# The second MLP product of a two-layer trunk with its seven block products as the outer loop

## The chip, the cores and the metric

The kernel runs on one core of a Trainium2 chip. The metric is the device time of one execution in microseconds, the median of three plain runs of the kernel before. A profiled execution of its own gives the trace.

## What is computed

The reference is a trunk of two residual layers over 1024 tokens of width 1024 in float32. Each layer is a mixer (gated DeltaNet and GLA in the first, Mamba-2 SSD and RWKV-7 in the second) followed by an MLP with a squared ReLU; a last RMSNorm ends it.

```python
for layer in range(DEPTH):                      # DEPTH = 2, D_MODEL = 1024, D_FF = 4096
    hn = _rmsnorm(h, norm_mix_w[layer])
    ...                                         # mix = even or odd mixer of hn
    h = h + mix.astype(h.dtype)
    h = h + _sqrelu_mlp(_rmsnorm(h, norm_mlp_w[layer]), mlp_w1[layer], mlp_w2[layer]).astype(h.dtype)
return _rmsnorm(h, final_norm_w)

def _sqrelu_mlp(h, w1, w2):
    return jnp.square(jax.nn.relu(h @ w1)) @ w2
```

The change is in the second product of the MLP, (1024 x 4096) times (4096 x 1024), in both layers, and in the normalisation that follows it.

## The kernel before

The program is written with a tile framework: tiles come from pools with a number of buffers for each tag, dependencies become semaphore waits, and the order of each engine's instructions is fixed when the program is built, by a list scheduler that goes by program order and by priority. Code in `with self.urgent()` gets the highest priority. Each engine executes its instructions in that order, and a waiting instruction holds all that stand behind it on its engine. All DMAs are issued from the SP queue, in order too (`load` and `store`, L156).

The second product uses a seven-product block scheme (Strassen-Winograd). The output, tokens by columns, is cut into 2 x 2 blocks of 512 x 512, and so are the factors: the contraction over 4096 rows is cut into halves (z in `down_rows`, alternating blocks of 128 rows). The left factors of the seven products, sums and differences of halves of the activations, were made by the first product (`up`) and lie transposed in DRAM as `d_s` (7 x 16 x 128 x 512). The right factors are the quarters of W2 (`quads`, tile tag w2) and, for products 5, 6, 7 and 4, running differences of them, made on VectorE in `right` (L1815), two instructions of 128 x 1024 each.

The contraction inside one block product, 2048 rows, is taken in four parts of 512 rows (b). One pair (b, i) is 48 matmuls of 128 x 128 by 128 x 512: 4 slices of 128 rows, 4 tiles of 128 tokens, 3 terms. The three terms come from the splitting of each float32 factor into a rounded high part and a remainder: `down_splits` (L1737) makes a tile of tag hn for each factor with one ScalarE cast and one VectorE difference for each of its two halves, urgent. The pool hn has four buffers, so two products' factors.

Before the change b is the outer loop (L1807) and the seven products, in the order 1, 2, 5, 6, 3, 7, 4, are the inner one. A PSUM group a (four banks of tag pm) sums products 1, 6, 7 and 4 of one b, a group c (two banks of tag pd and two of tag pt) takes 2, then 5 and 3. After each product `add` (L1793) adds the four banks on VectorE to a 512 x 512 block of h, which is in SBUF as eight tiles: four of tag hh, four of tag acc. Quarters of W2 are loaded once for each b, four loads of 1 MB, and the left factors seven times 1 MB; each 1 MB is two DMAs of 512 KB. sr has two buffers, w2 five.

The stage begins while `up` still runs. `down_start` (L1749) loads the factors of the first product, the raw left factor of the second (`early`) and two tiles of h. The pools of `down` (w2, sr, acc) lie where `up` had its own, so their loads wait for it. They then go out in this order (L1835 to L1850): right factor of product 2, two quarters, left factor of product 5, a quarter of h, left factor of product 6, a quarter of W2, the rest of h.

At the end (b = 3) the last product, 4, goes tile by tile through `seven` (L1537), and the generators `done` (L2047) finish the eight token tiles: the sum of squares (made by `add`), `rms` (its power on POOL, L188), the scaling by row and column, the store. In layer 0, `done` also transposes the normalised tile on TensorE in banks of tag pt and splits it for the next layer. In layer 1, `weigh` multiplies half of a tile by the norm's weights on POOL beforehand.

Of the kernel before, what the change touches and what calls it, by code (L numbers as in the profile page):

```python
# [8 lines left out]
FP32 = mybir.dt.float32  # L9
# [10 lines left out]
NT = SEQ // 128  # L20
# [19 lines left out]
class Trunk:  # L40
# [1708 lines left out]
    def down_start(self, W2, d_s, d_h, out):  # L1749

# [15 lines left out]
        out.extend((raw, h))  # L1766
        yield

    def down(self, M, W2, d_s, d_h, begun, weigh, done):


        *begun, h = begun
        for t in range(2, NT):
            h.append(self.big() if t < 4 else M[2].tile([128, D], FP32, tag="acc", name=self.name("acc"), bufs=4))
        rows = self.down_rows(W2)
        order = (1, 2, 5, 6, 3, 7, 4)

        def raw(m, src):
            t = fresh(m)
# [4 lines left out]
        def fresh(m):  # L1784
            tag, bufs = (("sr", 2), ("w2", 5))[m]
            return M[1 - m].tile([128, 4, 512], FP32, tag=tag, name=self.name(tag), bufs=bufs)

        split = self.down_splits
        ahead = {}

        ss = self.const.tile([128, NT, 2], FP32, tag="ssq", name=self.name("ssq"))

        def add(half, c, ps, last, tiles=range(4)):  # L1793
            for tt in tiles:
# [4 lines left out]
                if last:  # L1799
                    self.sum_sq(ss[:, t, c:c + 1], v)  # L1800
                    if half and c:
                        weigh(v)

        for b in range(4):
            quad = {}

            def quads(z, c):  # L1807
                if (z, c) not in quad:
                    quad[z, c] = raw(1, rows[b, z][:, :, c * 512:c * 512 + 512])
                return quad[z, c]  # L1810

            def left(i):
                return raw(0, d_s[i - 1, 4 * b:4 * b + 4].rearrange("j p t -> p j t"))

            def right(i):  # L1815
                if i in (1, 2, 3):
                    return quads(*((0, 0), (1, 0), (1, 1))[i - 1])
                if i == 5:
                    quad["x"] = fresh(1)
                    src = quads(0, 1), quads(0, 0)  # L1820
                elif i == 6:
                    src = quads(1, 1), quad["x"]
                elif i == 7:
                    src = quads(1, 1), quads(0, 1)
                else:
                    src = quads(1, 0), quad["x"]
                out = quads(0, 1) if i == 7 else quad["x"]
                for j in range(0, 4, 2):
                    self.tt(out[:, j:j + 2], src[0][:, j:j + 2], src[1][:, j:j + 2], SUB)
                return out  # L1830

            a = [self.pm() for _ in range(4)]
            c = None
            for n, i in enumerate(order):
                if not b and not n:  # L1835
                    def rest(half, q):
                        for t in range(max(2, 4 * half), 4 * half + 4):
                            cs = slice(q * 512, q * 512 + 512)
                            self.load(h[t][:, cs], d_h[t * 128:t * 128 + 128, cs])

                    l, r, early = begun
                    right(2), quads(0, 0), quads(0, 1)
                    ahead[5] = left(5)
                    rest(0, 0)
                    ahead[6] = left(6)
                    quads(1, 1)
                    for half, q in ((1, 1), (0, 1), (1, 0)):
                        rest(half, q)
                elif not b and n == 1:
                    l, r = split([early, right(2)])  # L1850
                else:
                    l, r = split([ahead.pop(i, None) or left(i), right(i)])
                if i in (2, 5):
                    c = [self.pd(), self.pd(), self.pt(), self.pt()]
                ps = c if i in (2, 5, 3) else a
                new = i in (1, 2, 5)
                if b == 3 and i == 4:
                    ends = [done(t, h[t], ss[:, t]) for t in range(NT)]
                    for e in ends[0:4]:
                        next(e)  # L1860
                    for tt in range(4):
                        self.seven(c[tt], l, r, 4, True, slice(tt * 128, tt * 128 + 128))
                        next(ends[tt], None)
                        add(1, 0, c, True, (tt,))
                        next(ends[4 + tt])
                    for e in ends[4:8]:
                        next(e, None)
                    continue
# [237 lines left out]
```

## Time and profile before

| | us |
|---|---|
| median of three plain runs | 2613.86 (2611.11 to 2621.36) |
| profiled execution | 2596.22 |
| its span, first to last instruction | 2594.5 |
| mean granted TensorE clock | 0.983 |
| second product, layer 0 | from about 912 to 1250 |
| second product, layer 1 | from about 2263 to the end |

The profile's page gives the busy time of each engine over the span; a table of stretches gives the same for any part of it, with the granted clock and the share and rate of the DMA engines. In a timeline each row is a run of like instructions, with its start, its duration and, in brackets, how long its engine had been idle before it and what ended that. A busy TensorE is not one at its peak, since matmuls overlap: the distance of their starts tells the pace.

### The profile page before, as it was taken

Reading aid. Unit: us, or ns where it says so; the run is one execution under the profiler, and the core shown is the slowest. Engines: PE = TensorE matmul, PEld = TensorE weight load, DVE = VectorE, ACT = ScalarE, POOL = GpSimd, SP = SyncE. Lnnn points to the kernel's source line nnn. Section 1 sums busy time; section 2 is a strip of 40 time slices with the busy share of each in tenths; the row PEclk is TensorE's granted clock in tenths of the full one; section 3 lists DMA queues with packets and bytes.
Section 4 is the critical chain, followed back from the end, with each engine's and each line's share of the span. In section 5 each row is a group of like instructions: output and inputs, shape, how many; then the busy total and the mean of one; then the engine's idle time right before and its main releaser. Section 6 shows DMA issues by size and latency. Waiting matters only on the chain. (4 is left out here: it accounts for less than half of the span.)

```text
span 2594.5 us, 39524 instructions
## 1 busy us (share of the span) xinstructions
PE 2495.4 (96%) x14230; PEld 2080.4 (80%) x14230; DVE 1756.8 (68%) x3033; ACT 1131.5 (44%) x2131; POOL 538.2 (21%) x546
## 2 busy tenths in 40 slices
PE   7999999999999989999899999998999999999998
PEld 6788898997787768887677788887897778778886
DVE  6677443447687778778366558777657677777877
ACT  5732344336544533334343333444437444533334
POOL 2020124302344200001031112245211434100001
PEclk9999999999999999999999899999999999999999
DMA  4556544645766674442235356667646766674432
GB/s 141 155 154 181 158 157 149 220 152 157 230 226 229 223 268 159 161 146 95 77 94 173 108 171 185 194 194 211 198 143 189 226 229 211 217 263 162 144 132 98
DMA packets 428965, 452.75 MB, mean 175 GB/s; under 512 B 55153, under 2 KB 301154, under 8 KB 428770
## 3 DMA queue, kind: packets, MB, share of 16 engines
q1 hardware_dynamic: 428770, 450.23, 54.2%
q8 instruction: 113, 1.85, 0.3%
q14 instruction: 82, 0.67, 0.1%
HBM read 304.84 MB, written 145.28 MB: 173 GB/s over the span
## 5 line engine op out<-in xcount | busy, mean ns | idle before, releaser
L161 PE MATMUL pd<-hn,whi 128*128 128x512 f32 x1216 | 409.8, 411 | 1.4 <-DVE cy L184 1.1
L161 PE MATMUL pd<-whi,hn 128*128 128x256 f32 (+2 forms) x2048 | 394.3, 289 | 6.7 <-ACT hn L171 4.0
L161 PEld LDWEIGHTS pd<-whi,hn 128*128 128x128 f32 x2048 | 322.6, 190 | 13.2 <-ACT hn L171 4.4
L1873 PE MATMUL pm<-hn,hn 128*128 128x512 f32 x1440 | 330.4, 389 | 0.0
L1873 PEld LDWEIGHTS pm<-hn,hn 128*128 128x128 f32 x1440 | 270.1, 188 | 56.8 <-DVE x L177 0.6
L161 PE MATMUL pd<-wlo,hn 128*128 128x256 f32 (+2 forms) x1024 | 294.7, 288 | 0.3 <-DVE wlo L177 0.2
L161 PEld LDWEIGHTS pd<-hn,whi 128*128 128x128 f32 x1216 | 224.1, 190 | 53.9 <-issue 7.8
L161 PE MATMUL pd<-hn,wlo 128*128 128x512 f32 x608 | 248.2, 408 | 0.0
L171 ACT CAST hn<-sr 128x1024 fp32r<-128x1024 f32 x104 | 108.7, 1047 | 316.1 <-PE pm L1873 181.3
L188 POOL TENSOR_TENSOR rs<-rs,mhalf 128x1 f32<-128x1 f32 x40 | 22.8, 571 | 883.1 <-DVE rs L177 671.0
L161 PEld LDWEIGHTS pd<-wlo,hn 128*128 128x128 f32 x1024 | 194.4, 190 | 2.3 <-DVE wlo L177 0.9
L177 DVE TENSOR_TENSOR wlo<-wst,whi 128x512 fp32r<-128x512 f32 (+2 forms) x172 | 122.8, 718 | 84.2 <-ACT whi L171 75.9
L171 ACT CAST whi<-wst 128x512 fp32r<-128x512 f32 (+2 forms) x172 | 106.5, 620 | 165.7 <-PE pd L161 121.5
L1537 PE MATMUL pm<-rf,whi 128*128 128x512 f32 x512 | 161.4, 396 | 10.1 <-DVE h L177 10.0
L1873 PE MATMUL pd<-hn,hn 128*128 128x512 f32 x576 | 150.5, 396 | 14.4 <-ACT hn L171 11.5
L1537 PE MATMUL pm<-hn,whi 128*128 128x512 f32 x512 | 162.9, 399 | 0.9 <-ACT whi L171 0.9
L1873 PE MATMUL pt<-hn,hn 128*128 128x512 f32 x576 | 149.2, 394 | 0.0
L1873 PEld LDWEIGHTS pd<-hn,hn 128*128 128x128 f32 x576 | 109.7, 192 | 40.1 <-ACT hn L171 12.8
L177 DVE TENSOR_TENSOR hn<-sr,hn 128x1024 fp32r<-128x1024 f32 x104 | 127.0, 1221 | 16.3 <-ACT hn L171 16.2
L161 PEld LDWEIGHTS pd<-hn,wlo 128*128 128x128 f32 x608 | 115.2, 189 | 28.2 <-issue 3.6
L177 DVE TENSOR_TENSOR hn<-w,hn 128x1024 fp32r<-128x1024 f32 x108 | 131.4, 1218 | 4.5 <-ACT hn L171 4.5
L1873 PEld LDWEIGHTS pt<-hn,hn 128*128 128x128 f32 x576 | 109.8, 191 | 23.2
(430 smaller groups left out, 4998.5 us busy)
## 6 DMA issues: line engine op xcount, KB each, us to landing
sr<-d_s SPq DMA_DIRECT2D x104, 512.0 KB
hh<-in_mlp_w_dram SPq DMA_DIRECT2D x64, 512.0 KB
d_s<-s SPq DMA_DIRECT2D x128, 256.0 KB
w<-in_mlp_w_dram SPq DMA_DIRECT2D x64, 512.0 KB
d_s<-x SPq DMA_DIRECT2D x64, 256.0 KB
hh<-d_rec SPq DMA_DIRECT2D x32, 512.0 KB
wst<-in_even_w_in_dram SPq DMA_DIRECT2D x56, 256.0 KB
wst<-in_odd_w_in_dram SPq DMA_DIRECT2D x52, 256.0 KB
```

The lines of the kernel that those rows point to most:

```text
L161: self.nc.tensor.matmul(out=out, lhsT=lhsT, rhs=rhs, start=start, stop=stop)
L171: self.nc.scalar.copy(out=out, in_=in_)
L177: (eng or self.nc.vector).tensor_tensor(out=out, in0=a, in1=b, op=op)
L188: self.nc.gpsimd.tensor_tensor(out=out, in0=in_, in1=self.mhalf.broadcast_to(list(in_.shape)), op=ALU.pow)
L1537: self.nc.tensor.matmul(out=ps, lhsT=wt[l][:, k, sl], rhs=x[r][:, k, :], start=start and k + j == 0, stop=k + j == n + 1, skip_group_check ...
L1873: self.nc.tensor.matmul(out=ps[tt], lhsT=l[x][:, k, sl], rhs=r[y][:, k, :], start=new and k + q == 0, stop=k + q == 5, skip_group_check=True)
```

## The change

The seven block products become the outer loop and the four parts b the inner one. A block product is summed over all four parts in PSUM (`start` only at b = 0), and only then added to h, or, for product 5, copied by ScalarE into four tiles u5 (buffers of tag wlo), to which product 7's group is added.

- Since b is inside, each quarter of W2 is loaded again for each block product that uses it: 36 loads of 1 MB a layer in place of 16; the left factors stay at 28. Product 5's differences are kept on chip in four tiles (tag x) for products 6 and 4, product 7's is made in place in a w2 buffer.
- One pool takes the place of three: sr 2, w2 3 and x 4 buffers of 8 KB a partition.
- h is no longer loaded at the start. `fetch` loads its first four tiles behind the third part of product 1, and the other four, into two x tiles, behind the second part of product 4, where u5 and the sums a are then added.
- The first four token tiles are finished (`done`) behind product 3 and no longer in the last product. In both layers the scaling is done in place, except for the half that `weigh` multiplied on POOL, now in layer 0 too (tiles 4 to 7). In layer 0 the store of h goes before the scaling, and the transposes of tiles 0 to 3 use banks of tag pm.

```diff
-    def down_start(self, W2, d_s, d_h, out):
+    def down_start(self, W2, d_s, out):
...
-            self.load(raw[-1], d_s[1, j:j + 2].rearrange("j p t -> p j t"))
-        h = [self.big() for _ in range(2)]
-        for i, x in enumerate(h):
-            self.load(x, d_h[i * 128:i * 128 + 128])
+            self.load(raw[-1], d_s[0, 4 + j:6 + j].rearrange("j p t -> p j t"))
...
+        def right(i, b):
+            quad = lambda z, c: raw("w2", rows[b, z][:, :, c * 512:c * 512 + 512])
+            if i in (1, 2, 3):
+                return quad(*((0, 0), (1, 0), (1, 1))[i - 1])
+            if i == 5:
+                src = quad(0, 1), quad(0, 0)
+                out = xs[b] = fresh("x")
+            elif i == 7:
+                src = quad(1, 1), quad(0, 1)
+                out = src[0]
+            else:
+                src = quad(1, 1 if i == 6 else 0), xs[b]
+                out = xs[b]
+            for j in range(0, 4, 2):
+                self.tt(out[:, j:j + 2], src[0][:, j:j + 2], src[1][:, j:j + 2], SUB)
+            return out
+
+        def fetch():
+            for t in range(len(h), len(h) + 4):
+                if t < 4:
+                    h.append(self.big())
+                else:
+                    if t % 2 == 0:
+                        two = fresh("x").rearrange("p (t k) c -> p t (k c)", t=2)
+                    h.append(two[:, t % 2])
+                self.load(h[t], d_h[t * 128:t * 128 + 128])
...
-        for b in range(4):
...
+        four = lambda: [self.pd(), self.pd(), self.pt(), self.pt()]
+        a, c, u5 = [self.pm() for _ in range(4)], None, []
+        *begun, early = begun
+        for i in (1, 2, 5, 6, 3, 7, 4):
+            if i in (2, 5, 4):
+                c = four()
+            ps, new = (c if i in (2, 5, 3, 4) else a), i in (1, 2, 5, 4)
+            for b in range(4):
+                if i > 1 or b > 1:
+                    l, r = self.down_splits([left(i, b), right(i, b)])
+                elif b:
+                    l, r = self.down_splits([early, right(i, b)])
                 else:
...
+                    l, r = begun
+                if i == 4 and b == 3:
+                    ends += [done(t, h[t], ss[:, t], weighed) for t in range(4, NT)]
                     for tt in range(4):
...
+                        self.seven(ps[tt], l, r, 4, False, slice(tt * 128, tt * 128 + 128))
+                        next(ends.pop(0), None)
+                        add(1, 0, ps, True, (tt,))
+                        next(ends[3])
+                    for e in ends:
                         next(e, None)
...
+                    break
...
+                if i == 1 and b == 2:
+                    fetch()
+                if i == 4 and b == 1:
+                    fetch()
+                    add(1, 1, u5, True)
+                    add(1, 0, a)
+            if i in (1, 2):
+                add(0, 0, ps, i == 2)
+            elif i == 5:
+                for tt in range(4):
+                    u5.append(self.w.tile([128, 560], FP32, tag="wlo", name=self.name("u5"))[:, 0:512])
+                    with self.urgent():
+                        self.cp(u5[tt], ps[tt])
+            elif i in (6, 3):
+                add(0, 1, ps, i == 3)
+                if i == 3:
+                    ends = [done(t, h[t], ss[:, t], weighed) for t in range(4)]
+                    for e in ends:
+                        next(e)
+            elif i == 7:
+                for x, y in zip(u5, ps):
+                    with self.urgent():
+                        self.tt(x, x, y, ADD)
...
+            def done(t, h, ss, weighed):
+                v, w = K.halves(h), K.halves(wn)
+                if layer == 0:
+                    K.store(d_h[rows(t)], h)
+                r = K.rms(v, ss)
+                y = []
+                for q, x in enumerate(v):
+                    if q and t in weighed:
+                        x = weighed[t]
+                        K.act(x, x, AF.Identity, scale=r)
+                    else:
+                        K.stt(x, x, r, w[q])
+                    y.append(x)
+                    if layer:
                         K.store(out[rows(t), q * 512:q * 512 + 512], x)
...
+                    K.transpose_split(y, hn[t // 4], t, bank=K.pm if t < 4 else K.pt)
+
+            def weigh(x):
+                y = x if layer else K.s2("y")
+                K.tt(y, x, K.halves(wn)[1], eng=K.nc.gpsimd)
+                return y
```

## Rows read from the trace of the kernel before

**Rows 1.** The page: span, and busy time and share of each engine.

```profile
span 2594.5 us, 39524 instructions
PE 2495.4 (96%) x14230; PEld 2080.4 (80%) x14230; DVE 1756.8 (68%) x3033; ACT 1131.5 (44%) x2131; POOL 538.2 (21%) x546
```

**Rows 2.** Stretches: length, busy PE, PEld, DVE, ACT, POOL, PE clock, DMA share, GB/s.

```profile
2400.00:2500.00 100.00, 100.00 (x443) 82.81 (x442) 80.20 (x85) 37.13 (x39) 0.00 (x0) 1.00 0.42 147
```

**Rows 3.** The chain that ended last, layer 1: start, duration, what.

```profile
2311.18 10.88 PE pm L1873 x48
...
2332.94 32.64 PE pm L1873 x144
```

**Rows 4.** Timeline of TensorE, layer 0, second to fourth product.

```profile
930.19 0.73 PE L1873 MATMUL pd<-hn,hn 128*128 128x512 f32 x2 [1.34 <-ACT hn L171]
...
946.90 1.22 PE L1873 MATMUL pd<-hn,hn 128*128 128x512 f32 x2 [5.18 <-ACT hn L171]
...
962.44 2.88 PE L1873 MATMUL pm<-hn,hn 128*128 128x512 f32 x12
```

**Rows 5.** Timeline of TensorE, layer 1, start of the third product.

```profile
2295.70 1.22 PE L1873 MATMUL pd<-hn,hn 128*128 128x512 f32 x2 [5.02 <-ACT hn L171]
```

**Rows 6.** Stretches at the beginning, layer 0 (first) and layer 1.

```profile
944.00:955.00 11.00, 6.71 (x16) 4.84 (x17) 11.00 (x11) 5.05 (x6) 0.00 (x0) 0.53 0.98 355
...
2280.00:2290.00 10.00, 10.00 (x46) 8.28 (x45) 3.52 (x5) 3.15 (x3) 0.00 (x0) 1.00 1.05 391
2290.00:2300.00 10.00, 3.59 (x9) 2.12 (x9) 10.00 (x11) 3.88 (x4) 0.00 (x0) 0.63 1.05 387
```

**Rows 7.** Timeline of the SP queue, layer 1: loads issued at the beginning.

```profile
2275.54 3.11 SPq L156 DMA_DIRECT2D w<-in_mlp_w_dram  x5
2278.75 2.24 SPq L156 DMA_DIRECT2D sr<-d_s  x4
...
2284.16 9.80 SPq L156 DMA_DIRECT2D acc<-d_m  x8
```

**Rows 8.** Timeline of VectorE, layer 1, ahead of the third product.

```profile
2288.68 0.69 DVE L177 TENSOR_TENSOR hh<-hh,pd 128x512 f32<-128x512 f32 x1 [6.25 <-PE pd L1873]
...
2293.35 3.49 DVE L177 TENSOR_TENSOR w<-w,w 128x1024 f32<-128x1024 f32 x3
```

**Rows 9.** Stretch at the end of layer 0's second product.

```profile
1223.00:1262.00 39.00, 28.33 (x135) 21.88 (x133) 24.66 (x45) 15.71 (x35) 8.34 (x10) 0.87 0.19 68
```

**Rows 10.** Timeline of TensorE in that stretch, the third tile's products.

```profile
1237.59 4.75 PE L1537 MATMUL pt<-hn,hn 128*128 128x512 f32 x12 [3.43 <-DVE hn L177]
```

**Rows 11.** Timeline of the last 17 us, TensorE and VectorE.

```profile
2577.58 5.60 PE L1537 MATMUL pt<-hn,hn 128*128 128x512 f32 x24
2577.76 1.74 DVE L184 SCALAR_TENSOR_TENSOR hh<-hh,rs,n4w 128x512 f32<-128x512 f32 x1
...
2587.58 0.68 DVE L177 TENSOR_TENSOR acc<-acc,pt 128x512 f32<-128x512 f32 x1
...
2590.18 0.75 DVE L184 SCALAR_TENSOR_TENSOR acc<-acc,rs,n4w 128x512 f32<-128x512 f32 x1 [0.73 <-POOL rs L188]
```

**Rows 12.** Groups in 2333 to 2556 us: count, busy us, mean ns, idle before.

```profile
L177 DVE TENSOR_TENSOR hn<-sr,hn 128x1024 fp32r<-128x1024 f32 x42 | 51.3, 1221 | 7.2 <-ACT hn L171 7.2
L177 DVE TENSOR_TENSOR w<-w,w 128x1024 f32<-128x1024 f32 x22 | 26.2, 1220 | 0.1
L177 DVE TENSOR_TENSOR hh<-hh,pm 128x512 f32<-128x512 f32 x24 | 16.4, 688 | 18.6 <-PE pm L1873 18.6
L171 ACT CAST hn<-sr 128x1024 fp32r<-128x1024 f32 x42 | 44.0, 1047 | 138.4 <-PE pm L1873 83.7 <-PE pt L1873 34.9 <-issue 19.8
```

**Rows 13.** Timeline of the SP queue, layer 1: a left factor loaded alone.

```profile
2402.87 11.75 SPq L156 DMA_DIRECT2D sr<-d_s  x4
```

**Rows 14.** Stretches around that load, and (last) of two loads at once.

```profile
2402.00:2404.00 2.00, 2.00 (x11) 1.65 (x10) 1.97 (x2) 0.15 (x1) 0.00 (x0) 1.00 0.09 6
2404.00:2408.00 4.00, 4.00 (x19) 3.34 (x18) 3.26 (x4) 0.00 (x0) 0.00 (x0) 1.00 0.72 259
...
2427.00:2433.00 6.00, 6.00 (x29) 4.95 (x28) 4.31 (x6) 2.10 (x3) 0.00 (x0) 1.00 0.92 343
```

More of the change, by code (lines that the diff above doesn't have):

```diff
@@ L1759, in down_start, with fresh, raw @@
             raw.append(heads(self.big(), 2))
-            self.load(raw[-1], d_s[1, j:j + 2].rearrange("j p t -> p j t"))
-        h = [self.big() for _ in range(2)]
-        for i, x in enumerate(h):
-            self.load(x, d_h[i * 128:i * 128 + 128])
+            self.load(raw[-1], d_s[0, 4 + j:6 + j].rearrange("j p t -> p j t"))
         yield
         out.extend(self.down_splits([t[:, 0:4], t[:, 4:8]]))
-        out.extend((raw, h))
+        out.append(raw)
         yield
     def down(self, M, W2, d_s, d_h, begun, weigh, done):
-        *begun, h = begun
-        for t in range(2, NT):
-            h.append(self.big() if t < 4 else M[2].tile([128, D], FP32, tag="acc", name=self.name("acc"), bufs=4))
         rows = self.down_rows(W2)
-        order = (1, 2, 5, 6, 3, 7, 4)
-        def raw(m, src):
-            t = fresh(m)
+        ss = self.const.tile([128, NT, 2], FP32, tag="ssq", name=self.name("ssq"))
+        h, xs, weighed = [], {}, {}
+        def fresh(tag):
+            return M.tile([128, 4, 512], FP32, tag=tag, name=self.name(tag), bufs={"sr": 2, "w2": 3, "x": 4}[tag])
+        def raw(tag, src):
+            t = fresh(tag)
             for j in range(0, 4, 2):
@@ L1782, in raw, with left, add @@
             return t
[L1784 to L1793, printed above, removed]
+        def left(i, b):
+            return raw("sr", d_s[i - 1, 4 * b:4 * b + 4].rearrange("j p t -> p j t"))
+        def right(i, b):
[23 more added lines that the diff above has]
+                self.load(h[t], d_h[t * 128:t * 128 + 128])
+        def add(half, c, ps, last=False, tiles=range(4)):
             for tt in tiles:
@@ L1801, in add @@
                     if half and c:
-                        weigh(v)
-        for b in range(4):
[L1805 to L1824, printed above, removed]
-                else:
[L1826 to L1860, printed above, removed]
-                    for tt in range(4):
[L1862 to L1866, printed above, removed]
@@ L1872, in down @@
                         for q, (x, y) in enumerate(((0, 0), (0, 1), (1, 0))):
[L1873 removed]
+                            self.nc.tensor.matmul(out=ps[tt], lhsT=l[x][:, k, sl], rhs=r[y][:, k, :], start=new and b + k + q == 0,
                                                   stop=k + q == 5, skip_group_check=True)
[L1875 to L1878 removed]
+                if i == 1 and b == 2:
[21 more added lines that the diff above has]
+                        self.tt(x, x, y, ADD)
 def first(K, pool, src, hnT, ap, d_gate):
@@ L2042, in build @@
                 with tc.tile_pool(name=f"out{layer}", bufs=1) as O:
-                    K.up(X, O, W1, B, d_s, d_x, K.down_start(W2, d_s, d_m, begun), last)
+                    K.up(X, O, W1, B, d_s, d_x, K.down_start(W2, d_s, begun), last)
             wn = norm(io["norm_mix_w"][1] if layer == 0 else io["final_norm_w"])
             hn = []
-            def done(t, h, ss):
-                v = K.halves(h)
-                if layer:
-                    r = K.rms(v, ss)
-                    for q, x in enumerate(v):
-                        if q and t >= 4:
-                            K.act(x, x, AF.Identity, scale=r)
-                        else:
-                            K.stt(x, x, r, K.halves(wn)[q])
-                        K.store(out[rows(t), q * 512:q * 512 + 512], x)
-                    yield
-                else:
-                    y = K.normed(v, wn, t % 2, ss=ss)
-                    K.store(d_h[rows(t)], h)
-                    yield
+            def done(t, h, ss, weighed):
[12 more added lines that the diff above has]
+                    if layer:
+                        K.store(out[rows(t), q * 512:q * 512 + 512], x)
+                yield
+                if layer == 0:
@@ L2072, in build @@
+            def weigh(x):
+                y = x if layer else K.s2("y")
+                K.tt(y, x, K.halves(wn)[1], eng=K.nc.gpsimd)
+                return y
+            with tc.tile_pool(name=f"down{layer}", bufs=1) as M:
+                K.down(M, W2, d_s, d_m, begun, weigh, done)
             hnT = hn
```

13 lines of the change are left out of this document (1 added, 12 removed).

## The prediction

> **What bounds the kernel now.** I read the page's busy rows first, then a table of stretches, then the timelines at both ends of the two stages that the change rewrites. TensorE is busy 96% of the span [rows 1], so a change pays only where TensorE waits. Inside the second product it doesn't wait at all: from 2400 to 2500 us it is busy in every microsecond at the full clock, while VectorE is at 0.80 and the DMA engines at 0.42 [rows 2]. Three products of 48 matmuls take 32.64 us, one takes 10.88 us [rows 3], or 0.2267 us a matmul. The seven products in four row blocks and two layers are 1344 matmuls a layer, and the change issues the same 1344. So the 304.6 us a layer stay; what can move are the two ends.
>
> The beginning. In layer 0 the second product begins 1.34 us late at 930.19 and ends at 946.90 - 5.18 = 941.72, that is 0.65 us over 10.88. The third (number 5) holds TensorE from 941.72 to 962.44, 20.72 us in place of 10.88 [rows 4]. Lost: 1.34 + 0.65 + 9.84 = 11.8 us. In layer 1 the third begins after a wait of 5.02 us, so TensorE was free from 2290.68 [rows 5], and the next product starts at 2311.18 [rows 3]: 20.5 - 10.88 = 9.6 us lost. The stretch tells why: DMA moves 355 to 391 GB/s at a share about 1, TensorE is busy 6.71 of 11 us, and the granted clock is 0.53, so part of it ran at the lower of the two levels [rows 6]. The queue lists what was asked for: right factors, left factors two products ahead, the last three quarters of h [rows 7]. And VectorE, in order, sat 6.25 us in front of an addition to h that needs the end of a product, with the differences for product 5 behind it [rows 8].
>
> The end. In layer 0, TensorE is busy 28.33 of the 39 us after 1223 at a mean clock of 0.87 [rows 9], and the products of the third tile wait 3.43 us for VectorE [rows 10]: transposes of finished tiles hold both pt banks that they need. In layer 1 TensorE ends at 2577.58 + 5.60 = 2583.18. The last tile's addition starts only at 2587.58, and its last scaling ends at 2590.18 + 0.75 = 2590.93 [rows 11].
>
> **The change part by part.**
>
> *Adding to h.* Before: 29 groups of four additions out of PSUM a layer, 116. After: 32 on VectorE (seven groups into h, one into u5) and 4 ScalarE copies. So 84 fewer at 0.688 us [rows 12], 58 us of VectorE a layer. It is worth nothing inside the stage, since VectorE is not what TensorE waits for there [rows 2]. The four copies cost nothing either: ScalarE idles 138.4 us before 42 casts of left factors, most of it until TensorE frees their buffer [rows 12], and these banks are wanted only one block product (43.5 us) later.
>
> *Start of the stage.* The second product, (1, b=1), needs the left factor that was loaded early and one right factor, as the second does now, so layer 0's 1.34 + 0.65 us stay (2.0 us). Layer 1 had no such wait; I allow 0.3 us. The third, (1, b=2), needs 2 MB and no differences. Behind 2275.54 [rows 7] that makes half a right factor plus 2 MB, 2.6e6 bytes; at 391 GB/s [rows 6] 6.7 us and some 2 us around the transfer (a lone megabyte is all there 5.1 us after its issue [rows 13, 14], and 2.7 us at 391 GB/s are the moving), so about 2284.5. Its first half then takes two casts of 1.05 and two differences of 1.22 us, some 3.5 us with the overlap [rows 12]: ready at 2288, 2.7 us ahead of 2290.7. The fourth comes behind h's first 2 MB: 4.2e6 bytes more, 10.7 us, 2295 against 2298 needed. Both are in time, and no addition to h stands on VectorE before the fourth product is over. Bounds: 0 regained if the DMA backlog is the same, 21.4 us if all goes. I take 11.8 + 9.6 - 2.0 - 0.3 = **19 us**.
>
> *More loads.* A layer's right factors grow from 16 loads of 1 MB to 36, and left ones stay at 28. Mean demand goes from 44 to 64 MB in 304.6 us, 151 to 220 GB/s (with h 234). The peak is in block products 5 and 7: 3 MB in 10.88 us is 289 GB/s, against the 391 that the trace sustains over 10 us [rows 6]. Queue: the loads stand on SP, which waits in order for buffers; 2 sr and 3 w2 buffers are now 1.5 products' worth of quads in these rounds. One product's loads take these 2 us plus 8.0 us at 391 GB/s, 10.0 us. A difference is 2 x 1.22 = 2.4 us, a split one cast and 4 x 1.22, 5.9 us [rows 12]. In round 7 the difference is written in place, so one of its two buffers is held for all three, 18.3 us, the other for 12.4; (18.3 + 12.4)/3 = 10.2 us a product, just under 10.88. Cost 0, thinly covered; the upper bound is in the rivals. On the near side the rows support the cover: in the steady part no cast waited for a DMA, and the 22 differences waited 0.1 us [rows 12].
>
> A rule that speaks against this: alone, one 1 MB left factor moves at a mean 259 GB/s over 4 us [rows 14]. The Trainium skill (DMA: Bandwidth & Descriptors, Bandwidth) gives 6.15 us for a 1 MB transfer. If a product's three loads went one after another by that figure, 18.5 us would stand against 10.88, an estimate from that page; the two loads that are in flight together here, 2 MB at 343 GB/s over 6 us [rows 14], say that they overlap.
>
> *h loaded late.* The first half is fetched during block product 1, used 21 us later; the second lands in x buffers freed by the split of product 4's first two blocks, used from its third on. Its additions and squares (8 x 0.688 us) fit VectorE's slack, 10.88 - 6 x 1.22 = 3.6 us a product over two products. Zero, with up to 5 us a layer if a load is late and VectorE, in order, holds the splits.
>
> *Normalising tiles 0 to 3 early* (behind product 3). In layer 0 the scaling is now in place, so VectorE must wait for the store of h to leave: a 512 KB store, 1.3 us at 391 GB/s plus the same 2 us. That is 3.3 us against 3.6 us of slack, once. I charge **2 us** for this and the former together (0 to 12).
>
> *End of layer 1.* Additions to h from the a sums, squares and POOL products move out of the last product, as do scalings of tiles 0 to 3, one of which still ran at 2577.76 [rows 11]. The last tile's own chain takes 2590.93 - 2587.58 = 3.35 us; now it starts 4.4 us after TensorE. Without the queue in front it can start at once, less 0.5 us for tile 6's scaling, which waits for POOL: **4 us** (0 to 4.4).
>
> *End of layer 0.* Idle 10.7 us plus some 3 us for the clock can be regained [rows 9]. Tiles 0 to 3 get pm banks for their transposes, so the products no longer wait for pt, and the next layer's first products can run beside the rest. Tiles 4 to 7 keep their chain, now with the wait for the store in it (+2 us). I take **8 us** (0 to 13.7).
>
> *u5 in four wlo buffers.* In layer 0 the next layer's weight pieces get these four only after block product 4's second block, some 25 us before they are used. Zero; if the pieces were late, 2 us each.
>
> Sum: 19 + 8 + 4 - 2 = 29 us. The profiled run took 2596.2 us (span 2594.5 and 1.7 around it), which becomes 2567. The median of the plain runs lies 17.6 us above it, and I carry the difference over: 2613.9 - 29 = **2585 us**.
>
> **The rivals.**
>
> *A. The start stays as it is.* DMA, not the order, is late: h's 2 MB go ahead of the loads that TensorE needs, or VectorE's order again puts a wait in front of a split. For it: the DMA share of 1 for 25 us. Against it: 3 MB are needed where before the third product came behind 6. Then 8 + 4 - 2 remain, 2604 us, inside 0.5%.
>
> *B. Rounds 5 and 7 run dry (slower).* Place: the three w2 buffers. If the order of instructions lets only one product's pair be in flight, a product takes the whole 18.3 us of load, difference and split, 7.4 us over 10.88, in 16 products of two layers: 118 us, 2613.9 - 29 + 118 = 2703 us. It decides from 29/16 = 1.8 us a product on, a cycle of 12.7 us. For it: a margin of only 0.7 us in the count above, and VectorE's in-order wait [rows 8]. Against it: DMA has 100 GB/s in hand, and every wait of the steady stage is for TensorE [rows 12].
>
> *C. Loads in sequence.* At 5 us for each lone megabyte (it is there within 5.1 us of its issue [rows 13, 14]) three loads would take 15 us, 4.1 over, 16 times: 66 us, 2613.9 - 29 + 66 = 2651 us. The rate of 343 GB/s for two loads at once [rows 14] speaks against it. The rule cited above from the Trainium skill (DMA: Bandwidth & Descriptors, Bandwidth) leads to this case.
>
> *D. More is regained:* everything at both ends, 21.4 + 13.7 + 4.4 = 39.5 us, 2574 us; part of the forecast's own range.
>
> **How the numbers follow.** Forecast with D: 0.70, between 2574 and 2598. A: 0.14. B: 0.11, most of it with partial stalls, 2620 to 2700. C: 0.05. What a measurement of this kernel can tell from no change is about 0.5%, 13 us. So faster 0.70, same 0.14, slower 0.16. The range runs from 2572, the whole of both ends, to 2608, which takes in A; what is left out is B and C.
>
> **What would show it.** Right: TensorE without a gap between 930 and the end of layer 0's stage but for the first 2 us; DMA near 290 GB/s in two stretches of 43 us a layer with TensorE still full; the last addition within 1 us of the last matmul; 494 MB in all. Wrong: casts or differences that wait for w2 loads in rounds 5 and 7, a lower granted clock there, or a third product that still starts 5 us late.

## The result, and the profile after

The changed kernel takes 2584.73 us (median of 6 runs, 2570.73 to 2587.84) beside 2612.49 us (6 runs, 2600.51 to 2621.36) for the kernel before on the same chip: a ratio of 0.989, 95% interval 0.9853 to 0.9927, or 27.8 us less. Forecast were 2585 us and 29 us less. So the time is right; whether its terms are right is another question, and two of them are not.

The page of the changed kernel: span, then busy time and share of each engine [rows 1].

```profile
span 2582.8 us, 39463 instructions
...
PE 2498.3 (97%) x14230; PEld 2082.4 (81%) x14230; DVE 1649.9 (64%) x2865; ACT 1135.5 (44%) x2139; POOL 547.9 (21%) x546
```

VectorE has 168 instructions fewer, additions that at 0.688 us make 116 us, and works 107 us less, since some of the others take longer; TensorE has the same 14230 matmuls. To place the gain I cut TensorE's timeline into stretches. The looped matmuls of the second product are 1296 a layer; *start* runs from the first of them to the 193rd (the end of up's last product lies in it), *loop* from there to the last, *end 0* from there to the 48th matmul of the next layer's projection, *end 1* from the last one to the end of the span; *mixer* is what follows end 0, up to the second layer's up product. All in us, from start times of matmuls in one profiled execution of each kernel:

```
               start0  loop0  end0    mixer  start1  loop1  end1
before          61.44 250.01  45.30  674.25   59.07 250.01  22.60
after           55.57 254.07  30.27  686.64   53.72 250.01  19.79
a_again         56.54 252.07  30.27  673.51   54.03 250.01  19.80
b_again         60.93 250.01  45.19  672.71   59.26 250.01  22.60
e1_pools        49.47 251.37  30.27  673.63   49.49 250.01  19.80
e2_pt           56.38 253.71  34.44  684.89   52.58 250.01  20.72
e3_before_pm    60.48 250.01  32.25  683.75   60.17 250.01  22.62
e4_h_early      56.00 250.75  30.24  685.61   54.20 250.01  19.81
e5_w2_two       55.78 256.74  30.27  674.25   54.09 257.46  19.69
e6_adds_late    56.67 250.01  30.24  671.20   53.80 250.01  19.80
e7_done_late    56.39 250.01  30.19  674.65   53.84 250.31  19.81
e8_dummy        57.66 256.16  29.78  682.66   54.88 254.07  20.51
e9_both         49.46 250.01  30.25  682.07   49.45 250.01  19.81
e11_pt_late     56.47 250.01  34.38  674.34   54.25 250.01  19.81
```

Without a wait a loop takes 250.01 us (1103 matmuls at 0.2267 us) and a start 49.46 (e9). From before to after: start0 -5.9, loop0 +4.1, end0 -15.0, start1 -5.4, end1 -2.8, together **-25.0 us**. The profiled pair differs by 11.7 us only, since its mixer, which the change doesn't touch, took 12.4 us more; the runs a_again and e3 show below that this is chance.

TensorE in the changed kernel at the two starts (timeline: start, length, engine, line, operation, tiles, count, idle time before in brackets and what ended it) [rows 4, 5]:

```profile
933.30 3.92 PE L1850 MATMUL pm<-hn,hn 128*128 128x512 f32 x9 [4.21 <-ACT hn L171]
...
2278.77 2.50 PE L1850 MATMUL pm<-hn,hn 128*128 128x512 f32 x5 [2.48 <-ACT hn L171]
```

It is now the *second* product that waits, 4.21 and 2.48 us; the third follows without a wait. The SP queue of the same kernel says why [rows 7]:

```profile
924.47 0.32 SPq L156 DMA_DIRECT2D d_s<-s  x1
928.42 0.90 SPq L156 DMA_DIRECT2D w<-in_mlp_w_dram  x2
...
2271.63 0.32 SPq L156 DMA_DIRECT2D d_s<-s  x1
2273.70 0.90 SPq L156 DMA_DIRECT2D w<-in_mlp_w_dram  x2
```

The first right factor is asked for 4.0 and 2.1 us behind the last store of s. In the kernel before, its first half left ahead of that store (layer 0):

```profile
923.37 0.39 SPq L156 DMA_DIRECT2D w<-in_mlp_w_dram  x1
...
926.05 0.32 SPq L156 DMA_DIRECT2D d_s<-s  x1
```

The waits of the changed kernel's queue from 924 to 929 us (us in total, times, longest) hold one for the landing of a store of s:

```profile
SPq L156 <- DMA d_s<-s: 2.5, 1, 2.5
```

Stretches of the changed kernel (length, busy PE, PEld, DVE, ACT, POOL, PE clock, DMA share, GB/s): just behind the first wait, while the loads of block products 5 and 7 of layer 0 run, the end of layer 0 [rows 2, 6, 9].

```profile
933.00:936.00 3.00, 2.70 (x7) 2.12 (x8) 2.48 (x3) 2.35 (x3) 0.00 (x0) 0.61 1.06 396
936.00:940.00 4.00, 4.00 (x16) 3.21 (x16) 3.66 (x4) 3.14 (x3) 0.00 (x0) 0.87 1.05 386
...
1000.00:1043.00 43.00, 43.00 (x192) 35.59 (x191) 34.42 (x32) 18.18 (x24) 0.00 (x0) 1.00 0.92 333
...
1130.00:1174.00 44.00, 44.00 (x196) 36.44 (x195) 34.79 (x43) 18.48 (x24) 3.94 (x4) 1.00 0.88 317
...
1221.00:1253.00 32.00, 31.57 (x169) 25.24 (x169) 17.30 (x34) 15.03 (x30) 3.84 (x10) 1.00 0.22 83
```

Behind the wait the mean granted clock is 0.61 and then 0.87, so part of these 7 us ran at the lower of the two levels, and the 4.21 us cost 6.1 in all. In the two long stretches TensorE is busy in every microsecond while DMA moves 333 and 317 GB/s. At the end of layer 0 it is busy 31.57 of 32 us at the full clock, where it was 28.33 of 39 at 0.87 [rows 9]: there is nothing left to gain there.

The groups of differences in the second layer's stage (count, busy us, mean ns, idle before) [rows 12]:

```profile
L177 DVE TENSOR_TENSOR x<-w,x 128x1024 f32<-128x1024 f32 x16 | 18.9, 1220 | 4.0 <-DMA w<-in_mlp_w_dram 3.9
L177 DVE TENSOR_TENSOR w<-w,w 128x1024 f32<-128x1024 f32 x8 | 9.8, 1223 | 6.9 <-DMA w<-in_mlp_w_dram 6.9
L177 DVE TENSOR_TENSOR x<-w,w 128x1024 f32<-128x1024 f32 x8 | 9.6, 1221 | 9.6 <-DMA w<-in_mlp_w_dram 9.6
```

VectorE does wait for right factors there, 20.4 us in the layer, and the loop still takes 250.01 us.

The one loss inside a loop is in layer 0, at block product 4. VectorE, then TensorE of the changed kernel [rows 8]:

```profile
1202.99 0.69 DVE L177 TENSOR_TENSOR x<-x,u 128x512 f32<-128x512 f32 x1 [2.42 <-DMA x<-d_m]
...
1204.20 1.46 DVE L177 TENSOR_TENSOR wlo<-wst,whi 128x512 fp32r<-128x512 f32 x1
...
1208.31 1.21 DVE L177 TENSOR_TENSOR hn<-x,hn 128x1024 fp32r<-128x1024 f32 x1
```

```profile
1207.04 0.39 PE L1850 MATMUL pd<-hn,hn 128*128 128x512 f32 x1
1209.57 2.05 PE L1850 MATMUL pd<-hn,hn 128*128 128x512 f32 x5 [2.15 <-DVE hn L177]
1211.42 2.53 PE L1850 MATMUL pt<-hn,hn 128*128 128x512 f32 x6
```

An addition to h waits for the load of h's second half; behind it in VectorE's order stand more additions, two splits of the next layer's weights, and only then the split that TensorE needs. After the wait the rows are longer, 2.53 us in place of 1.52.

The last matmuls and VectorE's last steps [rows 11]:

```profile
2568.66 5.60 PE L1537 MATMUL pt<-hn,hn 128*128 128x512 f32 x24
```

```profile
2575.18 0.75 DVE L184 SCALAR_TENSOR_TENSOR x<-x,rs,n4w 128x512 f32<-128x512 f32 x1 [0.73 <-POOL rs L188]
2575.85 0.68 DVE L177 TENSOR_TENSOR x<-x,pt 128x512 f32<-128x512 f32 x1
...
2578.46 0.75 DVE L184 SCALAR_TENSOR_TENSOR x<-x,rs,n4w 128x512 f32<-128x512 f32 x1 [0.73 <-POOL rs L188]
```

TensorE ends at 2574.26, the last addition starts 1.59 us later (4.40 before), and the last scaling still waits 0.73 us for POOL.

### The profile page after: what moved, and what is told of

Its sections match the earlier page's. It is cut to its first block, busy times and chain, and to the rows that moved or that the text cites. A ratio compares the mean times of both kernels' runs of the same rounds, so it can differ in the third digit from the quotient of the medians.

```text
span 2582.8 us, 39463 instructions
## 1 busy us (share of the span) xinstructions
PE 2498.3 (97%) x14230; PEld 2082.4 (81%) x14230; DVE 1649.9 (64%) x2865; ACT 1135.5 (44%) x2139; POOL 547.9 (21%) x546
## 2 busy tenths in 40 slices
DMA packets 447909, 492.60 MB, mean 191 GB/s; under 512 B 56177, under 2 KB 302178, under 8 KB 447714
## 5 line engine op out<-in xcount | busy, mean ns | idle before, releaser
L1850 PE MATMUL pm<-hn,hn 128*128 128x512 f32 x1152 | 266.9, 393 | 6.7 <-ACT hn L171 6.7
L1850 PEld LDWEIGHTS pm<-hn,hn 128*128 128x128 f32 x1152 | 218.1, 190 | 54.0 <-ACT hn L171 7.5
L1850 PE MATMUL pd<-hn,hn 128*128 128x512 f32 x720 | 183.6, 390 | 2.1 <-DVE hn L177 2.1
L1850 PE MATMUL pt<-hn,hn 128*128 128x512 f32 x720 | 183.7, 391 | 0.0
L1850 PEld LDWEIGHTS pd<-hn,hn 128*128 128x128 f32 x720 | 135.3, 188 | 30.7 <-DVE hn L177 2.6
L1850 PEld LDWEIGHTS pt<-hn,hn 128*128 128x128 f32 x720 | 136.0, 189 | 28.4
L1537 PEld LDWEIGHTS pm<-rf,whi 128*128 128x128 f32 x512 | 95.0, 188 | 36.8 <-ACT whi L171 12.2
```

The source lines that it names most:

```text
L1537: self.nc.tensor.matmul(out=ps, lhsT=wt[l][:, k, sl], rhs=x[r][:, k, :], start=start and k + j == 0, stop=k + j == n + 1, skip_group_check ...
L1850: self.nc.tensor.matmul(out=ps[tt], lhsT=l[x][:, k, sl], rhs=r[y][:, k, :], start=new and b + k + q == 0, stop=k + q == 5, skip_group_chec ...
```

## Experiments

Times of single runs differ by some 15 us with the mixer, so the small questions are answered from the stretches in the table.

**e1_pools: is it the pool that delays the first loads?** The change puts the three kinds of tiles into one pool, where the kernel before has three.

```diff
-            return M.tile([128, 4, 512], ...
+            return M[tag].tile([128, 4, 512], ...
-            with tc.tile_pool(name=f"down{layer}", bufs=1) as M:
+            with ExitStack() as ms:
+                M = {n: ms.enter_context(tc.tile_pool(name=f"{n}{layer}", bufs=1)) for n in ("w2", "sr", "x")}
```

> The changed kernel with its one pool cut into three (w2, sr, x), nothing else. In its trace the first w2 load of layer 0 goes out at 928.42 us, where the kernel before had it at 923.37, and the second product's first matmul starts at 933.30 after a wait of 4.21 us (layer 1: a wait of 2.48 us). Theory: a pool's loads wait until all memory under it is free, also that of the last stores of the first product, which only the x buffers lie on. Then the w2 loads go out some 4 to 5 us earlier, the waits fall to about 1.3 us in layer 0 and 0 in layer 1, and the time falls by 5 to 6 us. Rival: the loads wait behind the last stores in the SP queue anyway, then both waits stay and the time doesn't move.

Starts of 49.47 and 49.49 us, 6.1 and 4.2 less than after: both waits are gone. The SP queue of this kernel, then TensorE (first looped matmul at 911.35, against 912.11 after):

```profile
921.02 0.40 SPq L156 DMA_DIRECT2D w<-in_mlp_w_dram  x1
922.99 0.32 SPq L156 DMA_DIRECT2D d_s<-x  x1
923.72 0.32 SPq L156 DMA_DIRECT2D d_s<-s  x1
924.09 0.46 SPq L156 DMA_DIRECT2D w<-in_mlp_w_dram  x1
```

```profile
920.75 14.62 PE L1850 MATMUL pm<-hn,hn 128*128 128x512 f32 x63
```

The first half of the right factor leaves ahead of the last stores, the second 0.37 us behind them. 2568.56 us (5 runs), ratio 0.9867 (0.9828 to 0.9907). The queue has no wait for a store there. The two starts regain 10.3 us where 5 to 6 were expected, since layer 0's wait went whole and the matmuls behind no longer run at the lower clock (1.00 granted from 920 to 940 us). What the experiment shows is that one pool delays the loads and three don't. That one pool waits for the last stores because it takes over the memory of their tiles I infer from the 2.5 us above; it was not tried by itself.

**b_again: the kernel before once more,** unchanged.

> The kernel before, unchanged, profiled once more. Looked at: the second layer's mixer, from the 48th matmul of its projection to the first matmul of its MLP: 674.3 us in the trace of before and 686.6 us in that of after, which gave back 12 us of the gain at a lower granted clock. Theory: this is chance of the granted clock from execution to execution, so this trace differs from 674.3 by several us. Rival: the changed order of instructions made it, so this trace has 674 us within 1.

Its stretches agree with the first trace within 0.5 us, its mixer within 1.6 (672.71). The expectation of several microseconds there missed; by itself the run says nothing on the mixer.

**a_again: the kernel after once more,** unchanged.

> The kernel after once more, unchanged, for the 12.4 us that the second layer's mixer took more in its trace than in the trace before (686.6 against 674.3 us). If the order of the instructions makes it longer, it is 686.6 us again, within 1 us. If it is the granted clock of the single execution, it may be anywhere from 671 to 687 us, and the granted clock between 1400 and 1500 us goes with it.

The mixer took 673.51 us, 13.1 less than in the first trace of the same program. The stretch from 1400 to 1500 us, first of the kernel after, then of a_again:

```profile
1400.00:1500.00 100.00, 98.90 (x616) 76.45 (x615) 53.81 (x119) 35.48 (x77) 18.75 (x15) 0.80 0.36 107
```

```profile
1400.00:1500.00 100.00, 98.92 (x708) 76.22 (x706) 60.51 (x135) 39.91 (x86) 18.75 (x15) 0.93 0.43 127
```

TensorE is as busy in both; in the first the mean granted clock was 0.80, in the second 0.93, so more of the first ran at the lower level, and it did 616 matmuls for 708. e3, which has the order of the kernel before, took 683.75 us there. So the 12.4 us belong to the single execution, not to the change.

**e3_before_pm: the banks alone.** In the kernel before, transposes of tiles 0 to 3 get pm banks.

```diff
-                    K.transpose_split(y, hn[t // 4], t)
+                    K.transpose_split(y, hn[t // 4], t, bank=K.pm if t < 4 else K.pt)
```

> The kernel before with one thing of the change: the transposes of tiles 0 to 3 in pm banks. The same stretch, 45.3 us before. Theory of the banks: 32 to 36 us here. Rival, the early normalisation: it stays above 42 us, since the scalings of tiles 0 to 3 still stand on VectorE in the last product.

End 0 falls from 45.30 to 32.25 us. TensorE there, now without the wait of 3.43 us [rows 10]:

```profile
1228.70 1.04 PE L165 MATMUL pm<-ident,y 128*128 128x128 f32 x8
1229.49 3.01 PE L1537 MATMUL pt<-hn,hn 128*128 128x512 f32 x12
1232.34 1.04 PE L165 MATMUL pm<-ident,y 128*128 128x128 f32 x8
1233.13 2.99 PE L1537 MATMUL pt<-hn,hn 128*128 128x512 f32 x12
```

**e2_pt: everything but the banks.** The kernel after, pt banks for all transposes.

```diff
-                    K.transpose_split(y, hn[t // 4], t, bank=K.pm if t < 4 else K.pt)
+                    K.transpose_split(y, hn[t // 4], t, bank=K.pt)
```

> The changed kernel with the transposes of tiles 0 to 3 back in pt banks. Looked at: the stretch from the last of layer 0's looped second-product matmuls to the 48th matmul of the next layer's projection, 45.3 us before the change and 30.3 us after it. Theory: the pm banks make most of these 15 us, so it goes back to 40 to 45 us. Rival: the early normalisation of tiles 0 to 3 makes them (VectorE is free in the last product), so it stays at 30 to 33 us.

34.44 us, not 40 to 45: my theory, that the banks are most of this gain, fell. Banks alone give 13.1, the rest alone 10.9, both 15.0. Two causes cover nearly the same idle time. What the rest is, the next two runs were to ask.

**e7_done_late: scalings of tiles 0 to 3 back in the last product.**

```diff
-                    ends += [done(t, h[t], ss[:, t], weighed) for t in range(4, NT)]
+                    ends = [done(t, h[t], ss[:, t], weighed) for t in range(NT)]
+                    for e in ends[0:4]:
+                        next(e)
...
-                if i == 3:
-                    ends = [done(t, h[t], ss[:, t], weighed) for t in range(4)]
-                    for e in ends:
-                        next(e)
```

> The kernel after with the scalings of tiles 0 to 3 back in the last product, where the kernel before has them. Theory of the prediction, that the gain at the end of layer 1 comes from taking this work out of VectorE's last queue: the stretch from the last looped product to the end goes from 19.8 us back to 22 to 23 us, and at the end of layer 0 the stretch up to the next layer's 48th product goes from 30.3 to 32 to 35 us. Rival, that the gain comes from the additions to h that are now fewer: both stretches stay within 0.5 us of 19.8 and 30.3.

30.19 and 19.81 us, no change at either end, as the rival has it; but the run doesn't ask its question. VectorE's last scalings of tiles 0 to 3 in layer 0, one line each from the kernel before, the kernel after and this run:

```profile
1230.70 1.48 DVE L184 SCALAR_TENSOR_TENSOR y<-hh,rs,n4w 128x512 f32<-128x512 f32 x2
...
1154.34 1.42 DVE L184 SCALAR_TENSOR_TENSOR hh<-hh,rs,n4w 128x512 f32<-128x512 f32 x2 [0.44 <-POOL rs L188]
...
1177.81 2.73 DVE L184 SCALAR_TENSOR_TENSOR hh<-hh,rs,n4w 128x512 f32<-128x512 f32 x4
```

TensorE begins the last product's tiles at 1223.56, 1221.97 and 1221.81 us. So here the scalings, though written into the last product, still ran some 40 us ahead of it, where the list scheduler had put them, and some 50 us ahead in layer 1. What the early scalings are worth stays open.

**e11_pt_late: e2 and e7 together.**

> The kernel after with the pt banks for all eight tiles' transposes and the scalings of tiles 0 to 3 back in the last product, both as the kernel before has them. With the pt banks alone the stretch from the last looped product of layer 0 to the next layer's 48th product took 34.4 us, against 45.3 us in the kernel before. If the early scalings give those 11 us, the stretch goes back to 41 to 45 us here. If it is the lighter queue of VectorE and the cheaper second half of each row (fewer additions to h, the weights multiplied in on POOL), it stays at 33 to 36 us. The end of layer 1 stays at 19.8 us in both.

34.38 us, the 34.44 of e2 again. Here too the scalings ran ahead of the last product (the last of layer 0 at 1176.14), so this run repeats e2 and says nothing of them. TensorE at the end of layer 0:

```profile
1225.20 3.79 PE L1537 MATMUL pt<-hn,hn 128*128 128x512 f32 x16
1228.87 0.66 PE L165 MATMUL pt<-ident,hh 128*128 128x128 f32 x4
```

The third tile's products go ahead of the first transposes; in the kernel before they stood behind the transposes of two tiles and waited 3.43 us [rows 10]. In the changed kernel product 4's sums hold their banks from its first part on (`c = four()` stands ahead of the loop over b), so that with pt banks it is the transposes that wait. That this makes the 10.9 us is argued, not shown: fewer additions to h in the last product, the early scalings, scaling in place and the second halves that POOL and ScalarE scale came with it, and none was tried alone.

**e4_h_early: h's first half asked for ahead of the loop.**

```diff
+        fetch()
...
-                if i == 1 and b == 2:
-                    fetch()
```

> The changed kernel with h's first four tiles fetched ahead of the first block product and not behind its third part. Looked at: from the first to the 193rd of the second product's matmuls, 61.4 and 59.1 us in the two layers before the change, 55.6 and 53.7 after it. Theory: the 2 MB go ahead of the factors and add up to 2.1e6 bytes / 391 GB/s = 5.4 us a layer to the start. Rival: they are there before the pool's memory is free, for their buffers are not in it, and cost nothing; then loading h late gains only through the two tiles and more that lay in the pool before.

Start +0.4 and +0.5 us; the two traces of the unchanged kernel differ by 1.0. This run doesn't ask its question either. Loads of h's first half, in the kernel after and in this run:

```profile
879.73 0.32 SPq L156 DMA_DIRECT2D hh<-d_m  x1
...
912.71 0.42 SPq L156 DMA_DIRECT2D hh<-d_m  x1
```

```profile
882.02 0.32 SPq L156 DMA_DIRECT2D hh<-d_m  x1
...
914.89 0.42 SPq L156 DMA_DIRECT2D hh<-d_m  x1
```

Counted from the first looped matmul (912.11 and 914.28) they left at the same moments within 0.2 us, and nearly so in the kernel before (879.57 and 912.55, from 911.88). The place of `fetch` behind the third part is one in the program alone: the first half of h is as early as it was, and only the second half came later, at 1182.60 us where the kernel before asked for it from 935.70 on. What that gives the start no run shows.

**e5_w2_two: two buffers for right factors in place of three.**

```diff
-            ... bufs={"sr": 2, "w2": 3, "x": 4}[tag])
+            ... bufs={"sr": 2, "w2": 2, "x": 4}[tag])
```

> The changed kernel with two w2 buffers in place of three. It prices the rival of rounds that run dry. By the count of buffer time (18.3 and 12.4 us for a product's pair in round 7, 12.4 twice in round 5) two buffers allow a product every 15.4 us in round 7 and every 12.4 us in round 5, where TensorE needs 10.88: 4 x 4.5 + 4 x 1.5 = 24 us a layer more in the loop (254.1 and 250.0 us from the 193rd to the last looped matmul after the change). If it costs less than 5 us a layer, the count overstates and the rival was never near; if over 40 us, loads, differences and splits don't overlap as assumed.

Loop 0 takes 256.74 us (+2.7 against the trace after, +6.7 against a loop without waits), loop 1 257.46 (+7.5). TensorE in block product 7:

```profile
1143.27 22.15 PE L1850 MATMUL pm<-hn,hn 128*128 128x512 f32 x97
1166.42 8.91 PE L1850 MATMUL pm<-hn,hn 128*128 128x512 f32 x38 [1.01 <-DVE hn L177]
```

The place of rival B is real, its price was not: with a buffer less, a layer loses some 7 of the 24 us that the count gives.

**e6_adds_late: the additions behind the second fetch keep their place in VectorE's order** and no longer go ahead of the splits.

```diff
-                with self.urgent():
+                with self.urgent() if first else ExitStack():
...
-                    add(1, 1, u5, True)
-                    add(1, 0, a)
+                    add(1, 1, u5, True, first=False)
+                    add(1, 0, a, first=False)
```

> The changed kernel with the eight additions behind the second fetch of h at ordinary priority, no longer ahead of the splits. In layer 0 the loop lost 4.1 us at its last product: an addition waited 2.42 us for h's last tiles, and the splits stood behind it on VectorE, with squares and the next layer's weight splits. Theory: in order, the additions hold the splits, so the loop of layer 0 falls from 254.1 to 250 to 251.5 us; layer 1 stays at 250.0. Rival: the next layer's weight splits (urgent, four of 0.69 us) hold them, then it stays above 253.

Loop 0 takes 250.01 us. A wait for h is still there, of 0.47 us, but the split stands ahead of it (VectorE, layer 0):

```profile
1199.20 1.21 DVE L177 TENSOR_TENSOR hn<-sr,hn 128x1024 fp32r<-128x1024 f32 x1
1200.33 1.21 DVE L177 TENSOR_TENSOR hn<-x,hn 128x1024 fp32r<-128x1024 f32 x1
...
1206.32 0.69 DVE L177 TENSOR_TENSOR x<-x,u 128x512 f32<-128x512 f32 x1 [0.47 <-DMA x<-d_m]
```

In e7 too the loop takes 250.01 us, with a wait of 2.21 us for h on VectorE: there one more split went ahead of it.

```profile
1201.68 1.21 DVE L177 TENSOR_TENSOR hn<-sr,hn 128x1024 fp32r<-128x1024 f32 x1
1202.82 1.21 DVE L177 TENSOR_TENSOR hn<-x,hn 128x1024 fp32r<-128x1024 f32 x1
1206.24 0.69 DVE L177 TENSOR_TENSOR x<-x,u 128x512 f32<-128x512 f32 x1 [2.21 <-DMA x<-d_m]
```

It is not the wait that costs, but what is queued behind it.

**e8_dummy: the 84 saved additions put back,** as additions that nothing reads, so the work is more than the reference asks for.

```diff
+                if b < 3:
+                    for tt in range(4):
+                        self.tt(self.s2("dm"), self.wn[:, 0:512], self.wn[:, 512:1024], ADD)
```

> The changed kernel with 84 more additions of 128 x 512 on VectorE a layer, four after each of the first three parts of each block product, on data that nothing reads: the number that the sums in PSUM save. Theory: VectorE has room in the loop, so loop and start move by less than 1 us each, and the saved additions as such are worth nothing. Rival: the relief of VectorE is part of the gain, then loop or start grow by several us a layer.

Against the two traces of after: start0 +2.1 and +1.1, loop0 +2.1 and +4.1, start1 +1.2 and +0.9, loop1 +4.1 in both, that is 4 to 5 us a layer. Of a layer's 84 additions 67 ran between its first and its last looped matmul, 46 us of VectorE, and 17 ahead of them. In product 7 TensorE now waits for a split:

```profile
1173.20 9.13 PE L1850 MATMUL pm<-hn,hn 128*128 128x512 f32 x39 [0.77 <-DVE hn L177]
```

**e9_both: e1 and e6 together.**

> The kernel after with both mends at once: three pools (so that the second stage's first loads need not wait for the last store of the product before) and the two groups of additions to h behind the second fetch left in their place in VectorE's order. Theory, that the two losses are separate: 49.5 us from the first to the 193rd looped product of each layer, 250.0 us for the rest of the loop in layer 0, and a time of some 18 to 20 us under the kernel after, about 2565 us, ratio to the kernel before some 0.983. Rival, that loads which come earlier bring VectorE's wait for h back in another place: the rest of the loop stays at 251 to 254 us in one of the layers, and the time is that of the three pools alone, ratio 0.987.

Starts (49.46 and 49.45) and loops (250.01) are at their least and the ends as in the kernel after, so the six stretches are 39.4 us under the kernel before where after has 25.0. TensorE loses nothing in the stage until its last matmuls. Time 2571.71 us (6 runs, 2562.10 to 2578.09) beside 2606.34 (11 runs), ratio 0.9863, 0.9836 to 0.9889, or 34.6 us less. It was never run beside the kernel after, and the two ratios' intervals overlap; that it is faster than after by 14 us rests on the stretches, not on the times, which cannot tell the 0.983 expected here from the 0.987 of the rival either.

## Why the prediction was right, point by point

The terms were 19 + 8 + 4 - 2 = 29; the traces show 11.2 + 15.0 + 2.8 - 4.1 = 25.0. The sum came out because two misses of 7 to 8 us have opposite signs; that the medians differ by 27.8 us where 29 were forecast is luck.

**What bounds it: right.** The loop of before has no wait in it (250.01), and all that was gained lies at the ends. The losses of before were read well: 61.44 - 49.46 = 12.0 and 59.07 - 49.46 = 9.6 us, for 11.8 and 9.6.

**The start: 11.2 for 19; the step that failed is the second product.** That the third product would come in time is right; whether fewer loads ahead of it, the missing differences or VectorE's order did it was not tried apart, and h's first half has no part in it, since it left as early as before (shown with e4); the 2 MB that the prediction puts ahead of the fourth product were not in that place. The step "layer 0's 1.34 + 0.65 us stay; layer 1 had no such wait; I allow 0.3" took over from before the moment at which the first right factor is asked for. That load's buffer is now in the one new pool, and it left 4.0 and 2.1 us behind the last stores of s. The waits cost 6.1 and 4.3 us with the clock behind them, for the 2.3 charged: 8.1 us too little, which is the miss. e1 regains 21.5 us in all, the upper bound of the prediction (21.4). I had read the change of pools in the diff and costed only the number of buffers.

**More loads at no cost: right.** 492.60 MB for 494; 333 and 317 GB/s where 289 were reckoned, with TensorE full. Rivals B and C are not there: three loads of a product are 3.15 MB, 9.4 us at 333 GB/s, under 10.88. The Trainium skill (DMA: Bandwidth & Descriptors, Bandwidth) gives 6.15 us for a transfer of 1 MB issued from GpSimd. Three in sequence, an estimate from that figure of the Trainium skill, are 18.5 us. The Trainium skill doesn't say that loads go in sequence, and the trace's 333 GB/s for several at once speaks against it. My sign of rival B, differences that wait for w2 loads, was badly chosen: they waited 20.4 us in layer 1 and cost TensorE nothing (250.01 us). A sign has to be a wait of the engine that bounds.

**The loop: right mechanism, -4.1 for -2.** "If a load is late and VectorE, in order, holds the splits" is what happened, in layer 0 only, 4.1 us in one trace and 2.1 in the other, inside the 0 to 12.

**84 additions worth nothing: half right.** TensorE did not wait for VectorE in the loop of before, so the term in the sum is 0. But the new order brings its right factors in denser, and with 67 of the 84 put back in the stage it loses 4 to 5 us a layer (e8). Taking them out paid for a slot that the change itself needs; the thin cover of products 5 and 7 was VectorE's as well as the buffers'.

**End of layer 0: 15.0 for 8, beyond the bound of 13.7; the term was mis-sized.** I subtracted 2 us for the wait for the store and kept the chain of tiles 4 to 7. Neither shows: TensorE has no gap worth the name. The bound took 3 us for the clock. The mechanism named, banks, gives 13.1 by itself (e3), but the rest of the change gives 10.9 without it (e2, e11), for which the prediction has no term. Which part of the rest does so, the early scalings among them, stays open.

**End of layer 1: 2.8 for 4.** The last addition starts 1.59 us behind TensorE, not under 1, since it stands behind tile 6's scaling, which waits for POOL: 4.40 - 1.59 = 2.81. I had allowed 0.5 us for this. What gave the 2.81 us, the additions or the scalings that left the last product, no run shows: in e7 the scalings had not come back into it.

**Carried to the median: right.** The profiled pair differs by 11.7 us and the medians by 27.8; 12.4 of the 16.1 between them are the mixer's. The sum over the stretches that the change touches (25.0, in the second trace 25.7) is nearer the medians than the pair of spans.

## What to carry to other kernels

When a change puts buffers into another pool, ask for the first load into it not only what it needs but whose memory it takes over: here one pool in place of three put the first loads 2 to 4 us behind the last stores, where half of the first had gone ahead of them, and cost half of the start's gain. Where an engine works in order, a late load costs what stands behind the instruction that waits for it, so an instruction with slack should not be put ahead of the one that feeds the bound. Compare two traces stretch by stretch before you believe the difference of their spans. And where a scheduler orders the instructions, look in the trace whether an edit moved what it was to move before you read a null result: in e4, e7 and e11 it had not.

## What the runs showed of the hardware that I had not expected

In the second layer's mixer the same program took 673.5 us in one execution and 686.6 in another, with a granted clock of 0.93 and 0.80 between 1400 and 1500 us and TensorE busy 98.9% in both. Over 14 traces of 12 kernels the mixer took 671 to 675 or 682 to 687 us and nothing between. After a wait of 4.21 us the granted clock was 0.61 over the next 3 us and 0.87 over the 4 behind, which added 1.9 us to it. And the load stream held 333 GB/s over 43 us beside a TensorE that had no idle time.
